# Splits of reloaded activations and weights given to POOL, a later combination step, ACT-issued stores and an 18th operand place in a float32 transformer block

## The chip, the cores and the metric

The kernel runs on one core of a Trainium2 chip. The metric is the time of one execution in device microseconds (us). Engines are named as in the profile: PE multiplies matrices (PEld loads its stationary operand), DVE, ACT and POOL work elementwise, SP only issues DMAs, each engine has its own in-order queue.

## The reference, cut to what matters

One decoder block over 2048 tokens of width 1024, in float32:

```python
h = rmsnorm(x, norm_pre_mix);  proj = h @ w_in        # q, k, v, u, z, gate_a, gate_b
y_attn = dilated_attention(rope(q), rope(k), v)       # 3 dilations x 4 heads, softmax over the 3 results
y_gmlp = gelu(u) * spatial_mix(layernorm(gelu(z)))
merged = sigmoid(gate_a) * (y_attn @ w_branch_attn) + sigmoid(gate_b) * (y_gmlp @ w_branch_gmlp)
x = x + rmsnorm(merged @ w_out, norm_post_mix)
h = rmsnorm(x, norm_pre_mlp)
x = x + rmsnorm(relu(h @ w_mlp_in)**2 @ w_mlp_out, norm_post_mlp)
```

## The kernel before, in words

**Precision by splitting.** Each float32 operand is split into a high part (a copy rounded to the type that PE takes, fp32r) and a low part (the operand minus the high part), and a product is three matmuls: high by high, high by low, low by high (`mm3`, lines 94 to 97). The helper `split` (line 67) makes the two parts: the high one on ACT (line 70) or on POOL (line 72), the low one by a subtraction on DVE or POOL (line 78, or line 85 where it was put off until behind a product). `split_in` (line 87) first issues the load from SP (line 91).

**Order of the work.** PE's order is as the program writes it. The order of ACT, DVE, POOL and SP is set by a planner with its own costs, except in the first products of the MLP and from the end of its first stage on (`as_written`): there they too run in the order written. Queues are strictly in order: an instruction that waits holds back everything behind it on its engine.

**The attention stretch.** The projections u, z and the gates g are cut into steps (one step: the three matmuls of one k-tile, for 512 tokens), and a generator `filler` (line 474) hands these steps out between the pieces of 48 attention units, some nine steps a unit (line 714 on). Each unit: scores on PE, masked maximum on DVE, `nm` on DVE (line 604), exponentials on ACT (line 607), transposes on PE, their split `ph` by ACT and DVE (lines 632, 633), `pf` by ACT (line 640), the product `pv` on PE (line 646). The steps need hT, the transposed activations of a chunk of 512 tokens (two buffers, four chunks). Chunks 0 and 1 were written to DRAM and come back by `reload_h` (line 212), at the gate columns n = 7 of the second half and n = 0 of the first: four loads, each 128x1024, each split in a high part on ACT and a low one on DVE. The weights w of a column come by `load_w` (line 221): two raw tiles (two buffers), high part on POOL, low part on DVE.

**The combination.** After the last unit, `combine(c)` (line 657) weighs the three attention results of each chunk, in the order c = 2, 3, 0, 1: loads A (two buffers), small work on DVE, a multiplication on DVE (line 681), two additions of 128x1024 (lines 683 and 684; on DVE for c = 2, else on POOL), transposes on PE (line 689), a copy on ACT and a store of 'ya' (one buffer). Between the chunks PE runs 30, 20, 17 and 13 steps of the filler (line 745). When the last chunk's transposes are out, the space goes to wb, the branch weights, needed by the merge.

**The MLP, first stage.** It is computed by Strassen-Winograd products over pairs of hidden tiles q: seven products i = 1..7 instead of eight (`product`, line 1005). Sums of the weights by POOL (`add_a`, lines 987 to 990) are split by `split_a` into seven rotating buffers, in the order WL: yt0, yt1, yt2, gmlp, yt3, yt4, yt5. In the first products some yt tiles still hold sums of transposed activations (tt) on their way to DRAM (td). The results are squared and stored to s_d by `store_s` (line 1021): while `store_eng` is SP (the first products, lines 1170 to 1227), the store is issued from SP; later from ACT.

**The MLP, second stage.** Eight groups g of two pairs q; each group has eight blocks of tokens, each block seven products of six matmuls (`yproduct`, line 1545). A product uses an operand (B11, B21, T2, T3, T1, T4, B22: numbers 0 to 6) of both q's, split by `op_w2` (line 1295: high on ACT, low on POOL) into one of 17 rotating places of 128x2x512. Within a block's period the order on PE is: i=1 (operand 0), the block before's i=7 (3) and i=5 (4), i=2 (1), i=6 (2), the block before's i=4 (5) and i=3 (6). The next group's operand 0 is made in block nth = 3, POOL's sums of its raw weights in nth = 4 (`sum_w2`, six subtractions) and in the last block (`sum_w2_last`, two), and its operands 1 to 6 in the last block, operand u+1 after the product that last uses operand u (line 1604). POOL also forms four sums of the stored s per block (lines 1354 to 1357), ACT and DVE split them.

Of the kernel before, what the change touches and what calls it, by code (L numbers as in the profile page):

```python
# [8 lines left out]
F32 = mybir.dt.float32  # L9
F32R = mybir.dt.float32r  # L10
# [31 lines left out]
def block_kernel(ctx, tc, a, out):  # L42
# [169 lines left out]
    def reload_h(c):  # L212

        hT[c] = hp.tile([P, 2, KT, 512], F32R, name=f"hT_b{c}", tag="hT", bufs=2)
        for k in range(0, KT, 2):
            split_in(hT[c][:, :, k:k + 2], hT_d[c, :, k:k + 2, :], None, "act")

    def w_src(i, kk):
        return a["w_in"][i, :, kk * 4:(kk + 1) * 4, :]

    def load_w(i, name):

        w = wp.tile([P, 2, 2, 4, 256], F32R, name=name, tag="w", bufs=3)
        for kk in range(2):
            raw = wp.tile([P, 4, 256], F32, name=f"{name}_r{kk}", tag="raw", bufs=2)
            split_in(w[:, kk], w_src(i, kk), raw)
        return [w[:, 0], w[:, 1]]

    def wide_tiles(name):
# [236 lines left out]
    def want(q):  # L466
        if q < len(queue) and q not in loaded:
            wi, kind, n, half = queue[q]
            if kind == "z":
                loaded[q] = None if n else load_wide(wi, f"w_z{half}")  # L470
            else:
                loaded[q] = load_w(wi, f"w_{kind}{n}{half}")

    def filler():

# [181 lines left out]
    def combine(c):  # L657

        A = cb.tile([P, 4, 3, 264], F32, name=f"A_{c}", tag="cA", bufs=2)
        for g in range(3):  # L660
            sp.dma_start(A[:, :, g, :], att_d[g][c * 512:(c + 1) * 512, :].rearrange("(n p) e -> p n e", p=P))
        yield
        M = sm.tile([P, 4, 4], F32, name=f"M_{c}", tag="cM")
        dve.tensor_max(M, A[:, :, 0, 260:264], A[:, :, 1, 260:264])
        dve.tensor_max(M, M, A[:, :, 2, 260:264])
        E = sm.tile([P, 4, 3, 4], F32, name=f"E_{c}", tag="cE")
        for g in range(3):
            dve.tensor_sub(E[:, :, g, :], A[:, :, g, 260:264], M)
        act.activation(E, E, AF.Exp, scale=0.125)
        Z = sm.tile([P, 4, 3, 4], F32, name=f"Z_{c}", tag="cZ")  # L670
        for g in range(3):
            dve.tensor_mul(Z[:, :, g, :], E[:, :, g, :], A[:, :, g, 256:260])
        dve.tensor_add(M, Z[:, :, 0, :], Z[:, :, 1, :])
        dve.tensor_add(M, M, Z[:, :, 2, :])
        dve.reciprocal(M, M)
        for g in range(3):
            dve.tensor_mul(E[:, :, g, :], E[:, :, g, :], M)
        for i in range(4):
            for g in range(3):
                o = A[:, i, g, 0:256].rearrange("p (j e) -> p j e", j=4)  # L680
                dve.tensor_tensor(o, o, widen(E[:, i, g, :], 64), op=OP.mult)
        eng = dve if c == 2 else pool
        eng.tensor_add(A[:, :, 0, :256], A[:, :, 0, :256], A[:, :, 1, :256])
        eng.tensor_add(A[:, :, 0, :256], A[:, :, 0, :256], A[:, :, 2, :256])
        yield
        for m in range(2):
            pt = psum_aux(f"yt_{c}{m}")
            for i in range(4):
                pe.transpose(pt[:, i * P:(i + 1) * P], A[:, i, 0, m * P:(m + 1) * P], ident)
            yt = cb.tile([P, 512], F32, name=f"ya_{c}{m}", tag="cya", bufs=1)  # L690
            act.activation(yt, pt, AF.Copy)
            sp.dma_start(ya_d[m, :, c * 512:(c + 1) * 512], yt)
        yield
# [48 lines left out]
        next(cs[n])  # L742
        next(cs[n])
    for n in range(4):
        steps((30, 20, 17, 13)[n])
        next(cs[n])
        if n < 2:
            next(cs[n + 2])
            next(cs[n + 2])
# [255 lines left out]
    def product(half, q, i):  # L1005
# [13 lines left out]


        def store_s(o, t):
            (act if store_eng is None else store_eng).dma_start(s_d[q, half][:, :, o, :], t.rearrange("p (i c) -> p i c", i=4))

        def square(t, src):
            act.activation(t, src, AF.Relu)
# [267 lines left out]
        w2r_[q] = raw  # L1293

    def op_w2(q, name, lo_eng):
        w = spots[n_op[0] % 17]
        n_op[0] += 1
        raw = w2r_[q][:, dict(B11=0, B12=1, B21=2, T2=4, T3=1, T1=0, T4=2, B22=3)[name]]
        split(w[:, 0], w[:, 1], raw, "act", lo_eng)
        w2_[q, name] = w  # L1300

    def sum_w2(q, part):
# [59 lines left out]
            split(w[:, 0, :, to], w[:, 1, :, to], raw[:, :, k], "act", "dve")  # L1362
            yield

    def ops_of(g, j, lo_eng="pool"):
        ops = OPS if g < NQ // 2 - 1 else PLAIN_OPS
        for q in (2 * g, 2 * g + 1):
            if j < len(ops):
                op_w2(q, ops[j], lo_eng)

    last_ones = order[n_last:]

    def fours(name):
        w = bp.tile([P, 4, 2, 512], F32R, name=f"{name}_spots", tag=name, bufs=1)
        spots.extend(w[:, k] for k in range(4))

    in_order = behind()
    in_order.enter_context(as_written())
# [4 lines left out]
    for n, z in enumerate(last_ones):  # L1383
        if n == 0:
            for w in range(2):
                load_w2(w)
            load_s(0)
            load_s(1)
            split_a(h, q - 1, "S2", "S3")
        elif n == 1:  # L1390
            split_a(h, q - 1, "S1")
        elif n == 2:
            split_a(h, q - 1, "A22")
            add_a(h, q)
        elif n == 3:
            split_a(h, q - 1, "S4")
        elif n == 5:
            split_a(h, q, "S2")
        elif n == 6:
            split_a(h, q, "S3", "S1")  # L1400
        elif n == 7:
            split_a(h, q, "A22")
            next(s0)
        elif n == 8:
            split_a(h, q, "S4")
            rest()
            next(s0)
        elif n == 9:
            ew.close()
            s1p = stack(e3, "s1p", 1)  # L1410
            sm = stack(e3, "sm3", 2)
            acc0 = s1p.tile([P, D], F32, name="acc0")
            spots.append(s1p.tile([P, 2, 512], F32R, name="spot0"))
            fours("T2")
            for j in range(2):
                ops_of(0, j, "dve")
        elif n == 10:
            for part in (0, 1):
                for w in range(2):
                    sum_w2(w, part)  # L1420
            next(s0)
        elif n == 11:
            next(s0)
            rest()
            load_s(2)
        elif n == 12:
            fours("T3")
            ops_of(0, 2, "dve")
            next(s1)
        elif n == 13:  # L1430
            fours("T1")
            ops_of(0, 3, "dve")
            next(s1)
            for w in range(2):
                sum_w2_last(w)
        elif n == 14:
            fours("T4")
            ops_of(0, 4, "dve")
# [88 lines left out]
    def plain(n, k):  # L1527
# [7 lines left out]
        for m, q in enumerate((2 * g, 2 * g + 1)):  # L1535
            s, w = st_[n][:, :, m, at_], w2_[q, name]
            for o, (l, r) in enumerate(((0, 0), (0, 1), (1, 0))):
                pe.matmul(p, s[:, l], w[:, r], start=not t and not m and not o, stop=t == 1 and m == 1 and o == 2,
                          skip_group_check=True)
        if t:  # L1540
            an = acc[half, b, ci][:, nh * 512:(nh + 1) * 512]
# [3 lines left out]
    def yproduct(n, i):  # L1545
# [7 lines left out]
        for m, q in enumerate((2 * g, 2 * g + 1)):  # L1553
            s, w = st_[n][:, :, m, S_AT[i]], w2_[q, name]
            for o, (l, r) in enumerate(((0, 0), (0, 1), (1, 0))):
                pe.matmul(p, s[:, l], w[:, r], start=i in (1, 2, 5) and not m and not o, stop=m == 1 and o == 2,  # L1556
                          skip_group_check=True)
        ci, nh = {1: (0, 0), 2: (0, 0), 6: (0, 1), 3: (0, 1), 4: (1, 0), 7: (1, 1), 5: (1, 1)}[i]
        an = acc[half, b, ci][:, nh * 512:(nh + 1) * 512]
# [23 lines left out]
    for k, (_, n, i) in enumerate(yorder):  # L1583
# [4 lines left out]
        else:  # L1588
            yproduct(n, i)
        if not n and i in (1, 2):  # L1590
            ops_of(0, 4 + i, "dve")
# [113 lines left out]
```

## Time and profile before

| | |
|---|---|
| runs shown | 2780.45, 2775.97, 2776.09 us; median 2776.09 |
| profiled execution | 2779.44 us, its span 2777.7 us |
| PE busy | 2712.0 us of the span (98%) |
| DVE, ACT, POOL busy | 1545.2, 1051.9, 947.3 us |
| mean granted clock of PE | 0.991 |

Times of rows count from the span's start. A row of the timeline has start, duration, engine, line, operation, out<-in, shape, count, and in brackets the idle time of the engine before it and what ended that. A row of the waits has the total, the number and the longest of the waits. A row of the windows has the stretch, its length, then busy time and number of instructions for PE, PEld, DVE, ACT, POOL, the mean granted clock of PE (1.00 is full), and the share and rate of the DMA engines.

### The profile page before, as it was taken

To read this page: it belongs to the slowest core of one execution; us is meant where nothing else is said; L and a number is where in the kernel's file an instruction comes from. 1 tells how busy PE (TensorE), PEld (TensorE's weight loads), DVE (VectorE), ACT (ScalarE), POOL (GpSimd) and SP (SyncE) were. 2 spreads that over 40 slices of the span, in tenths; PEclk is the share of its full clock that TensorE was granted. 3 is DMA by queue.
4 is the path that set the end of the run, shared out by engine and by line. 5 is a ranking of instruction groups with operands and counts; after the bars stand their busy time and mean duration, and the time that the engine had idled before them with its cause. 6 is when DMAs were issued, how large, how long until landed. Compare 5 with 4: busy or idle time off the path is not lost. (4 is left out here: it accounts for less than half of the span.)

```text
span 2777.7 us, 34732 instructions
## 1 busy us (share of the span) xinstructions
PE 2712.0 (98%) x12668; PEld 2242.3 (81%) x12668; DVE 1545.2 (56%) x2643; ACT 1051.9 (38%) x2151; POOL 947.3 (34%) x777
## 2 busy tenths in 40 slices
PE   9999999999999999999999999999999999999998
PEld 7888888888878887787787788878887887777787
DVE  5655552344453344554556644555436777777766
ACT  5213111244453321354444544555444333233334
POOL 0341341200000013312215432223314766677645
PEclk9999999999999999999999999999999999999999
DMA  7445455466666654655658534554343122222236
GB/s 266 168 145 169 156 152 195 126 190 195 193 217 192 190 166 149 186 190 160 183 171 268 168 103 125 181 168 126 106 146 108 54 84 84 84 84 84 84 106 213
DMA packets 298380, 426.00 MB, mean 153 GB/s; under 512 B 18528, under 2 KB 172384, under 8 KB 298208
## 3 DMA queue, kind: packets, MB, share of 16 engines
q1 hardware_dynamic: 210368, 372.12, 42.3%
q10 hardware_dynamic: 87840, 51.65, 6.2%
q8 instruction: 100, 1.64, 0.2%
q14 instruction: 72, 0.59, 0.1%
HBM read 282.99 MB, written 140.71 MB: 153 GB/s over the span
## 5 line engine op out<-in xcount | busy, mean ns | idle before, releaser
L1556 PE MATMUL ya<-T_spots,s 128*128 128x512 f32 x1272 | 313.1, 392 | 4.8 <-DVE acc L1564 2.7
L1556 PEld LDWEIGHTS ya<-T_spots,s 128*128 128x128 f32 x1272 | 239.0, 188 | 59.0 <-issue 4.5
L70 ACT ACTIVATE s<-sraw 128x768 fp32r<-128x768 f32 (+1 forms) x184 | 126.0, 695 | 358.2 <-POOL sraw L1355 199.0
L1016 PE MATMUL aa<-B,A 128*128 128x512 f32 x768 | 187.0, 396 | 6.3 <-ACT xs L1030 5.1
L78 DVE TENSOR_TENSOR s<-sraw,s 128x512 fp32r<-128x512 f32 x171 | 163.6, 979 | 34.6 <-ACT s L70 33.0
L987 POOL TENSOR_TENSOR s<-w1r 128x512 f32<-128x512 f32 x32 | 43.5, 1359 | 397.3 <-DVE S L78 337.3
L1016 PEld LDWEIGHTS aa<-B,A 128*128 128x128 f32 x768 | 145.5, 190 | 40.5 <-ACT xs L1030 6.0
L72 POOL TENSOR_SCALAR w_g<-w_g_r 128x1024 fp32r<-128x1024 f32 x32 | 34.1, 1082 | 412.3 <-PE g L97 313.7
L1556 PE MATMUL yc<-T_spots,s 128*128 128x512 f32 x624 | 164.1, 394 | 3.6 <-POOL T_spots L78 3.6
L95 PE MATMUL x<-hT_a,wq 128*128 128x512 f32 x384 | 149.7, 390 | 0.0
L97 PE MATMUL x<-hT_a,wq 128*128 128x512 f32 x384 | 149.4, 389 | 0.0
L96 PE MATMUL x<-hT_a,wq 128*128 128x512 f32 x384 | 149.4, 389 | 0.0
L1556 PEld LDWEIGHTS yc<-T_spots,s 128*128 128x128 f32 x624 | 115.8, 188 | 33.6 <-POOL T_spots L78 9.7
L653 DVE TENSOR_REDUCE o<-po 128x256 f32<-128x512 f32 x48 | 33.1, 690 | 187.5 <-PE po L652 187.5
L78 POOL TENSOR_TENSOR T_spots<-w2r,T_spots 128x512 fp32r<-128x512 f32 x86 | 123.2, 1459 | 5.4 <-ACT T_spots L70 5.4
L70 ACT ACTIVATE hl<-r 128x512 fp32r<-128x512 f32 x48 | 30.4, 633 | 233.2 <-POOL r L287 89.0
L95 PE MATMUL g<-hT_b,w_g 128*128 128x512 f32 x256 | 105.0, 410 | 0.0
L95 PE MATMUL g<-hT_a,w_g 128*128 128x512 f32 x256 | 104.8, 409 | 0.0
L95 PE MATMUL o<-wo,mg 128*128 128x512 f32 x256 | 100.8, 394 | 4.1 <-ACT mg L70 4.1
L70 ACT ACTIVATE S<-w1r 128x512 fp32r<-128x512 f32 x96 | 60.0, 629 | 112.0 <-PE ac L1016 66.6
L815 POOL TENSOR_TENSOR g<-g,g 128x512 f32<-128x512 f32 x28 | 38.8, 1385 | 185.9 <-DVE g L813 179.2
L1354 POOL TENSOR_TENSOR sraw<-sraw 128x256 f32<-128x256 f32 x56 | 41.3, 737 | 174.6 <-DVE s L78 160.3
(379 smaller groups left out, 7214.4 us busy)
## 6 DMA issues: line engine op xcount, KB each, us to landing
w1r<-in_w_mlp_in_dram SPq DMA_DIRECT2D x64, 512.0 KB, 3.6
sraw<-sd SPq DMA_DIRECT2D x128, 256.0 KB, 3.4
qk<-hl SPq DMA_DIRECT2D x24, 1024.0 KB, 5.4
qq<-qk SPq DMA_DIRECT2D x96, 256.0 KB, 5.1
w_g_r<-in_w_in_dram SPq DMA_DIRECT2D x32, 512.0 KB, 5.3
gated<-gt SPq DMA_DIRECT2D x64, 256.0 KB, 3.4
g<-gated SPq DMA_DIRECT2D x64, 256.0 KB, 4.4
w2r<-in_w_mlp_out_dram SPq DMA_DIRECT2D x16, 1024.0 KB, 6.0
```

The lines of the kernel that those rows point to most:

```text
L70: act.activation(hi, src, AF.Copy)
L72: pool.tensor_scalar(hi, src, 1.0, 1.0, op0=OP.mult, op1=OP.mult)
L78: (pool if lo_eng == "pool" else dve).tensor_sub(lo, src, f32(hi))
L95: pe.matmul(ps, lh, rh, start=start, stop=False)
L96: pe.matmul(ps, lh, rl, start=False, stop=False)
L97: pe.matmul(ps, ll, rh, start=False, stop=stop)
L653: dve.tensor_reduce(ot[:, :, j * 64:(j + 1) * 64], po.rearrange("p (b h e) -> p b e h", b=4, h=2), axis=AX.X, op=OP.add)
L815: (dve if dt == KT - 1 else pool).tensor_add(parts[0], parts[0], parts[1])
L987: pool.tensor_add(s1, a21, a22)
L1016: pe.matmul(p, w[:, l, k, :], h[:, r, k, :], start=i in (1, 6, 5) and not k and not n, stop=k == 3 and n == 2, skip_group_check=True)
L1354: pool.tensor_add(a22, a21, a22)
L1556: pe.matmul(p, s[:, l], w[:, r], start=i in (1, 2, 5) and not m and not o, stop=m == 1 and o == 2, skip_group_check=True)
```

## The change

- `reload_h`: high and low part of the four pieces on POOL (were ACT and DVE).
- `load_w`: for the gate columns n = 0 and 1 of the first half, the low part on POOL too.
- `combine`: the two additions of chunk 1 on DVE (were on POOL); two buffers for 'ya'; the steps between the chunks are 33, 21, 20 and 24.
- `WL` begins with gmlp; the order is then yt0, yt1, yt2, yt3, yt4, yt5.
- `store_s` always issues from ACT.
- Second stage: an 18th place (two tiles of the buffers xs); operands 0 and 1 of the next group in block nth = 3; its eight sums in nth = 4 (one q) and nth = 5 (the other), none in the last block; in the last block operand u+2 after the last use of operand u; the low part of the first q on DVE for the operands made behind i = 2 and i = 7 (operands 3 and 5).

```diff
         for k in range(0, KT, 2):
-            split_in(hT[c][:, :, k:k + 2], hT_d[c, :, k:k + 2, :], None, "act")
+            split_in(hT[c][:, :, k:k + 2], hT_d[c, :, k:k + 2, :], None, "pool", "pool")
...
-    def load_w(i, name):
+    def load_w(i, name, lo_eng="dve"):
...
-            split_in(w[:, kk], w_src(i, kk), raw)
+            split_in(w[:, kk], w_src(i, kk), raw, "pool", lo_eng)
...
-                loaded[q] = load_w(wi, f"w_{kind}{n}{half}")
+                loaded[q] = load_w(wi, f"w_{kind}{n}{half}", "pool" if (kind, half) == ("g", 0) and n < 2 else "dve")
...
-        eng = dve if c == 2 else pool
+        eng = dve if c in (1, 2) else pool
...
-            yt = cb.tile([P, 512], F32, name=f"ya_{c}{m}", tag="cya", bufs=1)
+            yt = cb.tile([P, 512], F32, name=f"ya_{c}{m}", tag="cya", bufs=2)
...
-        steps((30, 20, 17, 13)[n])
+        steps((33, 21, 20, 24)[n])
...
-    WL, n_wl = ("yt0", "yt1", "yt2", "gmlp", "yt3", "yt4", "yt5"), [0]
+    WL, n_wl = ("gmlp", "yt0", "yt1", "yt2", "yt3", "yt4", "yt5"), [0]
...
-            (act if store_eng is None else store_eng).dma_start(s_d[q, half][:, :, o, :], t.rearrange("p (i c) -> p i c", i=4))
+            act.dma_start(s_d[q, half][:, :, o, :], t.rearrange("p (i c) -> p i c", i=4))
...
-        w = spots[n_op[0] % 17]
+        w = spots[n_op[0] % len(spots)]
...
-    def ops_of(g, j, lo_eng="pool"):
+    def ops_of(g, j, lo_engs=("pool", "pool")):
         ops = OPS if g < NQ // 2 - 1 else PLAIN_OPS
-        for q in (2 * g, 2 * g + 1):
+        for q, eng in zip((2 * g, 2 * g + 1), lo_engs):
             if j < len(ops):
-                op_w2(q, ops[j], lo_eng)
+                op_w2(q, ops[j], eng)
...
+    spots.append([rx.tile([P, 512], F32R, name=f"spot_{n}", tag="xs", bufs=LEAD + 1) for n in range(2)])
...
             if nth == 3:
                 ops_of(g + 1, 0)
-            if nth == 4 and g + 1 < NQ // 2 - 1:
+                ops_of(g + 1, 1)
+            if nth in (4, 5) and g + 1 < NQ // 2 - 1:
+                w = 2 * g + nth - 2
                 for part in (0, 1):
-                    for w in (2 * g + 2, 2 * g + 3):
-                        sum_w2(w, part)
+                    sum_w2(w, part)
+                sum_w2_last(w)
...
-        if more and nth == len(blocks) - 1 and USE[i][0] < 6:
-            ops_of(g + 1, USE[i][0] + 1)
-            if i == 1 and g + 1 < NQ // 2 - 1:
-                for w in (2 * g + 2, 2 * g + 3):
-                    sum_w2_last(w)
+        if more and nth == len(blocks) - 1 and USE[i][0] < 5:
+            ops_of(g + 1, USE[i][0] + 2, ("dve" if i in (2, 7) else "pool", "pool"))
```

The other changed lines only carry a place as a pair of tiles instead of one tile.

More of the change, by code (lines that the diff above doesn't have):

```diff
@@ L1295, in op_w2 @@
     def op_w2(q, name, lo_eng):
-        w = spots[n_op[0] % 17]
+        w = spots[n_op[0] % len(spots)]
         n_op[0] += 1
         raw = w2r_[q][:, dict(B11=0, B12=1, B21=2, T2=4, T3=1, T1=0, T4=2, B22=3)[name]]
-        split(w[:, 0], w[:, 1], raw, "act", lo_eng)
+        split(*w, raw, "act", lo_eng)
         w2_[q, name] = w
@@ L1374, in fours @@
         w = bp.tile([P, 4, 2, 512], F32R, name=f"{name}_spots", tag=name, bufs=1)
-        spots.extend(w[:, k] for k in range(4))
+        spots.extend((w[:, k, 0], w[:, k, 1]) for k in range(4))
     in_order = behind()
@@ L1412, in block_kernel @@
             acc0 = s1p.tile([P, D], F32, name="acc0")
-            spots.append(s1p.tile([P, 2, 512], F32R, name="spot0"))
+            w = s1p.tile([P, 2, 512], F32R, name="spot0")
+            spots.append((w[:, 0], w[:, 1]))
             fours("T2")
             for j in range(2):
-                ops_of(0, j, "dve")
+                ops_of(0, j, ("dve", "dve"))
         elif n == 10:
@@ L1427, in block_kernel @@
             fours("T3")
-            ops_of(0, 2, "dve")
+            ops_of(0, 2, ("dve", "dve"))
             next(s1)
@@ L1431, in block_kernel @@
             fours("T1")
-            ops_of(0, 3, "dve")
+            ops_of(0, 3, ("dve", "dve"))
             next(s1)
@@ L1437, in block_kernel @@
             fours("T4")
-            ops_of(0, 4, "dve")
+            ops_of(0, 4, ("dve", "dve"))
             next(s1)
@@ L1537, in plain @@
             for o, (l, r) in enumerate(((0, 0), (0, 1), (1, 0))):
-                pe.matmul(p, s[:, l], w[:, r], start=not t and not m and not o, stop=t == 1 and m == 1 and o == 2,
+                pe.matmul(p, s[:, l], w[r], start=not t and not m and not o, stop=t == 1 and m == 1 and o == 2,
                           skip_group_check=True)
@@ L1555, in yproduct @@
             for o, (l, r) in enumerate(((0, 0), (0, 1), (1, 0))):
-                pe.matmul(p, s[:, l], w[:, r], start=i in (1, 2, 5) and not m and not o, stop=m == 1 and o == 2,
+                pe.matmul(p, s[:, l], w[r], start=i in (1, 2, 5) and not m and not o, stop=m == 1 and o == 2,
                           skip_group_check=True)
@@ L1590, in block_kernel @@
         if not n and i in (1, 2):
-            ops_of(0, 4 + i, "dve")
+            ops_of(0, 4 + i, ("dve", "dve"))
         if i == 1 and more:
```

## The prediction

> **What bounds the kernel now.** First the page's busy times:
>
> ```profile
> PE 2712.0 (98%) x12668; PEld 2242.3 (81%) x12668; DVE 1545.2 (56%) x2643; ACT 1051.9 (38%) x2151; POOL 947.3 (34%) x777
> ```
>
> PE is the bound: nothing of its work is removed, so only its idle 2% and the time that it runs at a lower clock can be won. Then the waits of PE (who ended them; total, number, longest), and the windows of the four stretches that the change touches:
>
> ```profile
> PE yt L689 <- POOL A L684: 5.1, 1, 5.1
> ...
> PE yc L1556 <- POOL T_spots L78: 3.6, 5, 0.7
> ...
> PE pv L646 <- ACT ph L632: 2.7, 1, 2.7
> ...
> PE ya L1556 <- DVE acc_yt L1561: 2.1, 6, 0.4
> ```
>
> ```profile
> 765.00:800.00 35.00, 28.60 (x146) 24.14 (x145) 19.97 (x36) 19.61 (x46) 2.06 (x2) 0.90 0.71 234
> ...
> 1065.00:1080.00 15.00, 9.91 (x40) 8.11 (x39) 6.36 (x4) 1.68 (x3) 9.10 (x5) 0.77 0.44 139
> ...
> 1505.00:1545.00 40.00, 32.12 (x116) 23.83 (x116) 27.53 (x25) 21.63 (x33) 20.47 (x12) 0.87 0.85 273
> 2136.00:2755.00 619.00, 612.58 (x2661) 497.58 (x2660) 449.83 (x615) 202.80 (x381) 413.50 (x390) 1.00 0.30 97
> ```
>
> Length less PE busy is PE's idle time: 6.4, 5.1, 7.9 and 6.4 us. The clock column adds a second loss: after the first three PE ran part of the time at half clock; 0.90 of 35 us is 7 us at half. Of these stretches' half-speed time the part that falls into the wait itself is not lost again, so I count 3.0, 2.0 and 4 us. In all about 35 us are to be had.
>
> **A. Reload in the attention stretch** (`reload_h`, `load_w`).
>
> ```profile
> 765.81 1.06 ACT L70 ACTIVATE hT_b<-hT_b 128x1024 fp32r<-128x1024 f32 x1 [1.80 <-DMA hT_b<-hTd]
> ```
>
> ```profile
> 783.18 0.39 PE L95 MATMUL g<-hT_b,w_g 128*128 128x512 f32 x1
> ```
>
> ```profile
> 790.43 0.40 PE L95 MATMUL g<-hT_b,w_g 128*128 128x512 f32 x1
> ```
>
> ```profile
> 803.71 0.39 PE L95 MATMUL g<-hT_b,w_g 128*128 128x512 f32 x1
> ```
>
> ACT's four high parts stand among a unit's exponentials, `ph` comes late, PE waits for `pv`; but the first reload is not used before 783.18, its last quarter at 790.43, and the second, by the count of steps, at 803.71. With the splits on POOL this wait has no cause: +9.4 us (6.4 idle, 3.0 clock). POOL's price for a piece is one high part and one low:
>
> ```profile
> 744.05 2.06 POOL L72 TENSOR_SCALAR w_g<-w_g_r 128x1024 fp32r<-128x1024 f32 x2 [31.63 <-PE g L97]
> 783.43 2.06 POOL L72 TENSOR_SCALAR w_g<-w_g_r 128x1024 fp32r<-128x1024 f32 x2 [37.33 <-DMA qq<-qk]
> ```
>
> ```profile
> 1064.16 3.59 POOL L683 TENSOR_TENSOR A<-A 128x1024 f32<-128x1024 f32 x1 [4.49 <-DVE A L681]
> 1067.73 1.04 POOL L72 TENSOR_SCALAR w_z<-w_z_r 128x1024 fp32r<-128x1024 f32 x1
> 1068.73 2.34 POOL L684 TENSOR_TENSOR A<-A 128x1024 f32<-128x1024 f32 x1
> 1071.04 2.02 POOL L72 TENSOR_SCALAR wb<-wbraw 128x1024 fp32r<-128x1024 f32 x1
> ```
>
> That is 1.04 + 2.4 = 3.45 us beside an idle DVE, 2.02 + 3.59 = 5.6 beside a busy one. POOL is otherwise empty there. Ten pieces stand in a row: four of the first reload from 765.8 (where ACT gets the first now), two of the weights that now come at 783.43, four of the second reload. They end at 765.8 + 34.5 = 800.3. Needed: the first reload 6.7 us earlier than now, since 3.7 us of waits (2.7 of them the row of `ph`) and the 3.0 of slow clock before 783.18 are gone: from 776.5, last quarter 7.2 us on at 783.7; POOL has it at 779.6. The second 803.71 - 783.18 = 20.5 us later, less the stretch's other 2.7 us of waits: from 794.3, last quarter at 801.5. So POOL is in time by 1 us if the weights go first, and by more if not. What it may cost is DVE:
>
> ```profile
> 744.32 0.80 DVE L604 TENSOR_SCALAR nm<-o 128x4 f32<-128x4 f32 x1
> ```
>
> ```profile
> 753.93 0.17 DVE L604 TENSOR_SCALAR nm<-o 128x4 f32<-128x4 f32 x1
> ```
>
> ```profile
> 757.32 0.28 ACT L640 ACTIVATE pf<-pT 128x128 f32<-128x128 f32 x1 [0.49 <-DVE ph L633]
> ```
>
> ```profile
> 759.01 0.39 PE L646 MATMUL pv<-pf,v 128*128 128x128 f32 x2
> ```
>
> `nm` took 0.80 instead of 0.17 beside POOL's split, ending as POOL's first instruction did. Behind POOL's 2.4 us it can wait that long; exponentials, `ph` and `pf` queue behind it, and `pf` (done 757.60) has 1.4 us until PE uses it at 759.01. So at most 1.0 a unit, in five units, and only if it meets the wrong phase: 0.7 us. [...] SP's queue: raw tiles of these weights come free some 5 us later, SP's next weight loads with them; units' loads run two units ahead and hide it. I take +8; the ends are +9.4 and the rival below.
>
> **B. Combination.**
>
> ```profile
> 1043.66 1.04 PE L689 MATMUL yt<-ident,A 128*128 128x128 f32 x8
> ```
>
> ```profile
> 1026.52 1.22 DVE L683 TENSOR_TENSOR A<-A 128x1024 f32<-128x1024 f32 x1
> ```
>
> ```profile
> 1002.94 0.39 PE L97 MATMUL g<-hT_b,w_g 128*128 128x512 f32 x1
> ...
> 1003.62 0.39 PE L97 MATMUL g<-hT_b,w_g 128*128 128x512 f32 x1
> ```
>
> The chain that ends the 5.1 us wait: chunk 3's transposes (1043.66) free the buffer A, chunk 1 loads, DVE multiplies, POOL adds from 1064.16 to 1071.07: 27.4 us. Two adds on DVE take 2.4, and one weight split may stand between (1.2): done by about 1068, 24.4 us. PE's cover was 17 + 13 steps of 0.68 us (1002.94 to 1003.62) and two transposes, 22.4; it becomes 20 + 24 steps, 32. The wait goes, with 7 us to spare: +7.1 (5.1 idle, 2.0 clock); chunk 0 gets 41 steps where 37 sufficed. The second 'ya' buffer only frees ACT. Ending later costs the branch weights 18 steps, 12 us less the 5 saved:
>
> ```profile
> L78 DVE TENSOR_TENSOR wb<-wbraw,wb x6: 1225/1226/1227, 1073.1 to 1094.7; 128x1024 fp32r<-128x1024 f32 x6
> ```
>
> ```profile
> 1132.70 0.40 PE L95 MATMUL b<-yt,wb 128*128 128x512 f32 x1
> ```
>
> They were ready 37 us before use; hidden. I take +7 (5 to 7.5).
>
> **C. First products of the MLP** (`WL`, `store_s`).
>
> ```profile
> 1506.32 0.63 ACT L70 ACTIVATE S<-w1r 128x512 fp32r<-128x512 f32 x1 [1.39 <-DMA td<-tt]
> ...
> 1514.07 0.60 ACT L1025 ACTIVATE c<-aa 128x512 f32<-128x512 f32 x1 [4.38 <-DMA sd<-c]
> ...
> 1517.85 0.63 ACT L70 ACTIVATE A<-ar 128x512 fp32r<-128x512 f32 x1 [0.63 <-DMA ar<-in_w_mlp_in_dram]
> ```
>
> ```profile
> 1507.00 0.73 PE L1016 MATMUL ab<-T_first,S 128*128 128x512 f32 x2 [1.12 <-ACT S L70]
> ...
> 1519.02 1.22 PE L1016 MATMUL aa<-B,A 128*128 128x512 f32 x2 [3.99 <-ACT xs L1030]
> 1521.48 4.54 PE L1016 MATMUL aa<-B,A 128*128 128x512 f32 x10 [1.23 <-DVE A L85]
> ```
>
> ```profile
> 1510.63 0.91 SPq L946 DMA_DIRECT2D ar<-in_w_mlp_in_dram  x1
> ```
>
> ```profile
> 1543.75 0.54 ACTq L1022 DMA_DIRECT2D sd<-u  x1
> ```
>
> S in gmlp no longer waits for a td store (1.39), and c no longer for SP to get to its store (4.38). But then the product of 1519.02 is held by its weights: 'ar' lands at 1517.8, 7.2 us after its issue, with the DMA engines 0.85 busy, and that stays. PE reaches this product earlier and waits longer; its low part is done near 1519.5 instead of 1521.4. Seven stores on ACT cost 0.54 each, 3.8 us, most of it in ACT's gaps. I take +2. Ends: -3.8 (no store hidden) and +10 (nothing waits, clock included).
>
> ```profile
> 1509.00:1512.00 3.00, 3.00 (x8) 2.31 (x7) 2.43 (x2) 0.63 (x1) 1.89 (x2) 0.50 0.93 285
> ```
>
> Half clock follows already on the 1.5 us wait of 1507 (1.12 and 0.38). [...]
>
> **D. Second stage.**
>
> ```profile
> 2201.21 3.00 POOL L1314 TENSOR_TENSOR w2r<-w2r 128x512 f32<-128x512 f32 x2
> ...
> 2213.87 8.73 POOL L78 TENSOR_TENSOR T_spots<-w2r,T_spots 128x512 fp32r<-128x512 f32 x6
> ```
>
> At each change of group POOL has twelve low parts of 1.46 us (six of them in the 8.73 us) and two sums of 1.5 close behind one another; PE waits 0.72 for operand 4, and 0.35 as the late s sums hold DVE. Six changes of group: 6.4 us, at full clock. After: eight low parts, no sums, and operand 4 four slots earlier: 4 x 1.46 + 3.0 = 8.8 us less, against 0.72. The two low parts on DVE wait 0.6 us for ACT there. Blocks 3, 4 and 5 now hold four low parts, four and four sums: 6 us each in a block of 9.7, where before block 4 held six sums, 9; hidden. +6 (3 to 6.4).
>
> **Sum.** 8 + 7 + 2 + 6 = 23. From the profiled 2779.4 that is 2756.4; this execution lies 3.3 above the median of the runs, 2776.1, so I forecast **2753**.
>
> **Rivals.**
> - *POOL becomes the bound in the attention stretch* (slower). If every piece costs 5.6 as beside a busy DVE, the tenth ends at 821.8, 20 us late, with 3.4 for half clock (6.8 us of it after the wait) and six units' `nm` held 3.59 - 1.4 = 2.2 each (13): A is 9.4 - 36.6 = -27, the sum -12: **2788**. It eats the whole gain from a piece of 4.7 us on (11 late, 3.4, and six times 1.6: A is -15, what B, C and D bring). For: the 3.59 row. Against: DVE has few two-input jobs there once these splits are gone. 0.08. [...]
> - *The second reload is a little late*: pieces of 4.0 us, 4.6 us late and half clock: A near 0, **2761**. For: a margin of 1 us. 0.12.
> - *ACT pays for the stores*: C at -3.8, **2759**. 0.07.
> - *The early products gain in full*, 'ar' landing earlier once two stores leave SP's queue ahead of it: C +10, **2745**. Against: the DMA engines are busy either way. 0.10.
> - *The waits only change their owner* (DVE's low parts hold the sums in D, planner's order undoes A): B alone, less new half-clock time, **2772**. 0.08.
>
> **Numbers.** The forecast, 2748 to 2758, has 0.55. Range 2744 to 2767: the four nearest cases; it leaves out 0.16 and little else. What a measurement here tells from no change is about 0.2%, 5.5 us: faster 0.84, within 0.08, slower 0.08.
>
> **What would show it.** A: no wait for `pv` near 770 and 795, POOL's ten pieces near 3.5 us, hT ready before use. B: no wait for yt. C: no wait for td or sd on ACT, one longer wait for 'ar'. D: no 0.7 waits of yc. Wrong if POOL's low parts take over 4 us, if PE waits for hT, or if the granted clock falls in a place where it is 1.00 now.

## The result, and the profile after

The changed kernel takes 2753.64 us (median of five runs, 2750.45 to 2756.65), the kernel before 2780.42 (median of five, 2775.97 to 2780.65): a ratio of 0.9907, 95% interval 0.9896 to 0.9917. The forecast was 2753.0. That it is met so closely is partly luck, as shown below: the terms of the sum came to 23 us, the change is worth 26 (25.8 by the profiled spans, 26.8 by the medians), and I had taken 3 us off for a base that was not there. The ratios here are of fast executions: three slow ones among those below, one of the kernel before (3827.9 us), one of C alone (6945.34) and one of D alone (3712.83), are left out of them.

The profiled execution of the changed kernel took 2753.64 us, its span 2751.9; that of before 2779.44 and 2777.7. So the spans differ by 25.8 us, and these are what the following rows have to account for. The page's busy times of the changed kernel:

```profile
PE 2699.0 (98%) x12668; PEld 2237.4 (81%) x12668; DVE 1558.8 (57%) x2646; ACT 1050.3 (38%) x2145; POOL 965.5 (35%) x782
```

PE has the same 12668 matmuls in 13 us less of busy time: half of the gain lies inside busy time; the other half is idle time. Of PE's busy time 38.65 us lay at half clock before and 20.22 after, by estimate 9 of the 13 us, counting a microsecond at half clock as half lost (in the changed kernel, matmuls of `g` start 0.43 us apart at 786.53 and 0.23 at 788.48); the rest I put down, as an estimate too, to pauses too short to count as idle, like those in a row of 1.79 us for six matmuls that take 1.52 elsewhere. The windows of the four stretches, first before, then after (columns as above; the combination before stands in the prediction; the third and the fourth window lie 13 and 14 us earlier after the change, as the work in them does):

```profile
757.00:800.00 43.00, 36.60 (x194) 31.16 (x193) 23.05 (x48) 21.68 (x50) 2.06 (x2) 0.92 0.70 224
...
1503.00:1553.00 50.00, 42.12 (x159) 32.01 (x158) 34.58 (x36) 27.70 (x43) 25.25 (x16) 0.90 0.85 278
2125.00:2744.00 619.00, 609.91 (x2643) 494.95 (x2642) 453.70 (x620) 204.81 (x375) 411.39 (x388) 1.00 0.30 96
```

```profile
757.00:800.00 43.00, 39.55 (x220) 33.99 (x219) 17.80 (x50) 17.47 (x54) 31.15 (x18) 0.96 0.76 239
1065.00:1080.00 15.00, 15.00 (x72) 12.52 (x71) 6.89 (x7) 2.28 (x4) 4.40 (x2) 1.00 0.53 179
1490.00:1540.00 50.00, 42.61 (x172) 32.90 (x171) 37.57 (x38) 30.16 (x48) 26.01 (x17) 0.93 0.79 267
2111.00:2730.00 619.00, 615.73 (x2690) 504.67 (x2689) 485.49 (x641) 212.98 (x393) 398.95 (x380) 1.00 0.30 99
```

Read them stretch by stretch: the combination (second row after) has no idle time and full clock; in the attention stretch (first) 3.45 us of idle time and a clock of 0.96 are left; in the first products of the MLP (third) 7.4 of 7.9 us of idle time are left, in three listed waits instead of six; in the second stage idle time fell from 9.1 to 3.3 us.

Where the time came from is read best from one and the same instruction in both timelines. Three such pairs, the first of each pair from before, the second from after:

```profile
808.72 0.69 DVE L653 TENSOR_REDUCE o<-po 128x256 f32<-128x512 f32 x1 [3.98 <-PE po L652]
...
1088.27 0.39 PE L95 MATMUL z<-w_z,hT_b 128*128 128x512 f32 x1
...
2138.33 0.85 PE L1556 MATMUL yc<-T_spots,s 128*128 128x512 f32 x3
```

```profile
803.27 0.69 DVE L653 TENSOR_REDUCE o<-po 128x256 f32<-128x512 f32 x1 [3.46 <-PE po L652]
...
1074.83 0.39 PE L95 MATMUL z<-w_z,hT_b 128*128 128x512 f32 x1
...
2122.65 1.54 PE L1558 MATMUL yc<-T_spots,s 128*128 128x512 f32 x6
```

Behind the attention stretch the changed kernel is 5.45 us ahead, behind the combination 13.44, early in the second stage 15.68, at the end 25.8. Part A gave 5.4 (forecast 8), B 8.0 (7), what lies between z and the second stage 2.2 (C was 2), D 10.1 (6).

The same rows in the other traces tell which of these numbers are the part's own. B's 8.0 and D's 10.1 come again, to 0.1 us, in every trace of a kernel with that part. A's 5.4 does not: in three of the other traces with the same A the reduction stands at 804.10 (a second trace of the changed kernel), 801.87 and 805.20 (the two runs under "Pieces of B and D", the second first), a lead of 4.6, 6.8 and 3.5 us. Nor are the 2.2 us C's own. The lead is 14.24 us ahead of the first products of the MLP (`pt`, line 868, at 1475.79 and 1461.55) and 16.18 behind them (`ac`, line 1016, at 1558.24 and 1542.06), so 1.9 us were won there; by the same rows it is 0.4 us in a second trace of the changed kernel and -0.3 in the run with C alone.

### The profile page after: what moved, and what is told of

Same layout as the page of the kernel before. It is cut to its first block, busy times and chain, and to the rows that moved or that the text cites. A ratio compares the mean times of both kernels' runs of the same rounds, so it can differ in the third digit from the quotient of the medians.

```text
span 2751.9 us, 34711 instructions
## 1 busy us (share of the span) xinstructions
PE 2699.0 (98%) x12668; PEld 2237.4 (81%) x12668; DVE 1558.8 (57%) x2646; ACT 1050.3 (38%) x2145; POOL 965.5 (35%) x782
## 5 line engine op out<-in xcount | busy, mean ns | idle before, releaser
L1558 PE MATMUL ya<-T_spots,s 128*128 128x512 f32 x1176 | 291.6, 391 | 3.3 <-DVE acc L1566 3.3
L1558 PEld LDWEIGHTS ya<-T_spots,s 128*128 128x128 f32 x1176 | 220.7, 188 | 52.3 <-ACT T_spots L70 3.1
L78 DVE TENSOR_TENSOR s<-sraw,s 128x512 fp32r<-128x512 f32 x171 | 179.6, 1075 | 7.1 <-ACT s L70 7.0
L78 POOL TENSOR_TENSOR T_spots<-w2r,T_spots 128x512 fp32r<-128x512 f32 x70 | 104.6, 1521 | 7.5 <-ACT T_spots L70 7.5
```

Source lines behind the costliest of these rows:

```text
L78: (pool if lo_eng == "pool" else dve).tensor_sub(lo, src, f32(hi))
L1558: pe.matmul(p, s[:, l], w[r], start=i in (1, 2, 5) and not m and not o, stop=m == 1 and o == 2, skip_group_check=True)
```

## Experiments

### Each part alone

**A alone.** The kernel before with `reload_h` and `load_w` as in the change:

```diff
-            split_in(hT[c][:, :, k:k + 2], hT_d[c, :, k:k + 2, :], None, "act")
+            split_in(hT[c][:, :, k:k + 2], hT_d[c, :, k:k + 2, :], None, "pool", "pool")
...
-                loaded[q] = load_w(wi, f"w_{kind}{n}{half}")
+                loaded[q] = load_w(wi, f"w_{kind}{n}{half}", "pool" if (kind, half) == ("g", 0) and n < 2 else "dve")
```

> The kernel before with part A alone (splits of the reload on POOL, low parts of gate columns 0 and 1 of the first half on POOL). Theory 1, four separate waits: the whole gain of A is 5.3 us (the idle time and slow clock near 770 and 795 less a new wait of PE for the transposes of a unit of 3.4 us near 784), so 2775 against 2780, and no other place of the trace moves. Theory 2, the parts need one another (the earlier steps of A are lost again at the combination, where the filler's steps cover a wait): 0 to 2 us, and the wait for yt longer than 5.1.

Measured: 2776.09 us against 2780.3, ratio 0.9988 (0.9980 to 0.9997). Of its waits of PE:

```profile
PE pT L627 <- DVE o L653: 5.0, 2, 4.3
PE yt L689 <- POOL A L684: 4.6, 1, 4.6
```

The new wait for the transposes (`pT`, 4.3 us here) is A's own, and the wait of the combination stays as it was: theory 1, with a gain at the lower end of what its trace says (the reduction of the row above stands at 804.16, 4.6 us earlier than before).

**B alone.**

```diff
-        eng = dve if c == 2 else pool
+        eng = dve if c in (1, 2) else pool
...
-            yt = cb.tile([P, 512], F32, name=f"ya_{c}{m}", tag="cya", bufs=1)
+            yt = cb.tile([P, 512], F32, name=f"ya_{c}{m}", tag="cya", bufs=2)
...
-        steps((30, 20, 17, 13)[n])
+        steps((33, 21, 20, 24)[n])
```

> The kernel before with part B alone (two additions of chunk 1 on DVE, two buffers for ya, steps 33, 21, 20, 24). Theory 1: 8 us less, 2772; no wait for yt, clock 1.00 between 1065 and 1080, the first product with the branch weights 8 us earlier. Theory 2, the 24 steps held back only move the wait to the branch weights or the first merge: 0 to 4 us, with a longer wait for g or wb behind it.

Measured: 2771.1 us, ratio 0.9969 (0.9957 to 0.9981). The window of the combination:

```profile
1065.00:1080.00 15.00, 15.00 (x72) 12.53 (x71) 13.91 (x30) 5.08 (x9) 5.88 (x2) 1.00 0.55 178
```

No idle time, full clock; theory 1.

**C alone.**

```diff
-    WL, n_wl = ("yt0", "yt1", "yt2", "gmlp", "yt3", "yt4", "yt5"), [0]
+    WL, n_wl = ("gmlp", "yt0", "yt1", "yt2", "yt3", "yt4", "yt5"), [0]
...
-            (act if store_eng is None else store_eng).dma_start(s_d[q, half][:, :, o, :], t.rearrange("p (i c) -> p i c", i=4))
+            act.dma_start(s_d[q, half][:, :, o, :], t.rearrange("p (i c) -> p i c", i=4))
```

> The kernel before with part C alone (WL begins with gmlp, first stores from ACT). Theory 1: 2 us less, inside what one kernel's runs scatter; one wait of about 5.7 us for xs near 1515 (ACT held by the landing of 'ar') in place of waits of 1.1, 4.0 and 1.2. Theory 2, the saving in C needs the other parts: no less than 0.5 us different from before.

Measured: 2777.64 us, ratio 0.9989 (0.9980 to 0.9998). One long wait for xs, 6.6 us, as expected, but waits for S of 0.8 twice are left in this run. The trace shows no saving at the place of C: it is 1.4 us ahead of the kernel before when the first products begin and 1.1 behind them. What the interval allows, 0.6 to 5.6 us, is thus not shown to be C's.

**D alone.** The second stage's part of the change, on the kernel before; its core:

```diff
-        w = spots[n_op[0] % 17]
+        w = spots[n_op[0] % len(spots)]
...
+                ops_of(g + 1, 1)
...
-            ops_of(g + 1, USE[i][0] + 1)
+            ops_of(g + 1, USE[i][0] + 2, ("dve" if i in (2, 7) else "pool", "pool"))
```

> The kernel with part D alone (second stage: 18th place, operands 0 and 1 and the sums early, two low parts on DVE). Theory 1, the trace's own account by periods of blocks: 10 us less, 2770, since a change of group costs 1.9 us before and nothing after, less 0.035 us a block. Theory 2, the sum of the listed waits, as I predicted: 6 us less, 2774, and the other 4 come from somewhere else (the end of the first stage, A to C).

Measured: 2769.09 us, ratio 0.9962 (0.9949 to 0.9975), that is 11 us: the account by periods, not the sum of the listed waits. The four ratios fall short of 1 by 0.12, 0.31, 0.11 and 0.38%, together 0.92%; the whole change by 0.93%. As far as intervals of about 0.1% each can tell, the parts are independent, and the rival that waits only change their owner is out.

### What is left of A

The wait of 3.4 us that the changed kernel has in the attention stretch, in its timeline (DVE, POOL, PE, in this order):

```profile
780.29 4.04 DVE L78 TENSOR_TENSOR w_g<-w_g_r,w_g 128x1024 fp32r<-128x1024 f32 x2 [4.79 <-POOL w_g L72]
784.25 0.68 DVE L653 TENSOR_REDUCE o<-po 128x256 f32<-128x512 f32 x1
```

```profile
779.21 2.06 POOL L72 TENSOR_SCALAR w_g<-w_g_r 128x1024 fp32r<-128x1024 f32 x2
781.24 2.01 POOL L72 TENSOR_SCALAR hT_b<-hT_b 128x1024 fp32r<-128x1024 f32 x1
783.33 3.21 POOL L78 TENSOR_TENSOR hT_b<-hT_b 128x1024 fp32r<-128x1024 f32 x1
...
794.65 2.40 POOL L78 TENSOR_TENSOR hT_b<-hT_b 128x1024 fp32r<-128x1024 f32 x1
```

```profile
784.98 0.90 PE L627 MATMUL pT<-ident,e 128*128 128x128 f32 x3 [3.44 <-DVE o L653]
```

Two low parts of weights took DVE 4.04 us instead of 3.18 before, side by side with POOL's splits of the second reload, which took 2.01 and 3.21 instead of 1.04 and 2.4. The reduction stands behind them in DVE's queue, PE's transposes wait for it. It stood there before too, and PE did not wait:

```profile
784.52 3.18 DVE L78 TENSOR_TENSOR w_g<-w_g_r,w_g 128x1024 fp32r<-128x1024 f32 x2 [1.66 <-POOL w_g L72]
787.63 0.68 DVE L653 TENSOR_REDUCE o<-po 128x256 f32<-128x512 f32 x1
```

The 0.9 us by which the low parts became longer are the smaller part of the wait. PE begins these transposes 7.3 us earlier than before (780.94 against 788.28), the two low parts only 4.2 us earlier (780.29 against 784.52): their high parts stood in POOL's queue behind the first reload, whose last piece ended at 779.2. The experiment takes those two low parts to POOL as well:

```diff
-"pool" if (kind, half) == ("g", 0) and n < 2 else "dve"
+"pool" if (kind, half) == ("g", 0) and n < 3 else "dve"
```

> The changed kernel with the low parts of gate column n = 2 on POOL too (n < 3 in place of n < 2): the ten pieces in a row that my prediction counted. Theory 1 (what is left of A's gain is lost to DVE, whose two weight splits took 4.04 us beside POOL's and stand ahead of the reduction that PE's transposes wait for): the wait of 3.4 us and the half clock behind it go, 4 to 5 us less than the changed kernel, about 2749; POOL's tenth piece ends near 800 against a need of 801.5. Theory 2 (POOL is then late): PE waits for hT near 796 to 800, and the time is that of the changed kernel or up to 4 us more.

Measured: 2748.95 us, ratio to before 0.9883 (0.9866 to 0.9899). Window, POOL, DVE and the same reduction as above:

```profile
757.00:800.00 43.00, 42.97 (x251) 37.15 (x250) 18.04 (x55) 18.25 (x55) 33.82 (x20) 1.00 0.87 273
```

```profile
781.52 4.76 POOL L78 TENSOR_TENSOR w_g<-w_g_r,w_g 128x1024 fp32r<-128x1024 f32 x2
```

```profile
781.57 2.37 DVE L604 TENSOR_SCALAR nm<-o 128x4 f32<-128x4 f32 x1
...
798.73 0.69 DVE L653 TENSOR_REDUCE o<-po 128x256 f32<-128x512 f32 x1 [2.71 <-PE po L652]
```

PE is busy for all 43 us at full clock, and the reduction comes 4.54 us earlier than in the changed kernel: theory 1. The row of `nm` shows POOL's price: an instruction that takes 0.17 us at 800.69 took 2.37 here, beside POOL's low part of 781.52. Nothing waited for it long enough to be seen on PE.

**Low parts of the reload on DVE.** The other way to relieve the meeting of the two engines:

```diff
-            split_in(hT[c][:, :, k:k + 2], hT_d[c, :, k:k + 2, :], None, "pool", "pool")
+            split_in(hT[c][:, :, k:k + 2], hT_d[c, :, k:k + 2, :], None, "pool", "dve")
```

> The changed kernel with the eight low parts of the reload back on DVE, the high ones staying on POOL. Theory 1 (DVE's queue is what PE waits for in this stretch, so work must leave DVE, not only ACT): DVE has 8 x 1.22 to 2.05 us more in the units; the wait for the transposes (3.4) comes back longer or at more places, 2 to 6 us more than the changed kernel, 2756 to 2760. Theory 2 (ACT's high parts alone made the old waits, the low parts may be anywhere): within 1 us of the changed kernel, or 1 to 3 us less since POOL's instructions that block DVE are shorter.

Measured: 2758.28 us (2754.16 to 2759.22), ratio 0.9916 (0.9901 to 0.9930), an interval that overlaps that of the changed kernel. The profiled run is the fastest of the four; its window and waits:

```profile
757.00:800.00 43.00, 39.92 (x225) 33.63 (x224) 26.61 (x59) 17.55 (x54) 12.63 (x10) 1.00 0.81 245
```

```profile
PE pT L627 <- DVE o L653: 2.3, 2, 1.7
PE pv L646 <- DVE ph L633: 1.5, 2, 1.2
```

In the stretch it loses as much as the changed kernel (3.1 us idle against 3.45), in two shorter waits and without half clock; its reduction stands at 802.68, 0.6 us earlier. Theory 2 holds for the stretch. The median falls into the 2756 to 2760 of theory 1, but nothing in the trace speaks for it; whether the median's 4.6 us more are real, and where they would lie, stays open. Against the ten pieces the picture is clear: the low parts belong on POOL, if all of them go there.

### What is left of C

In the changed kernel, PE and ACT at the one long wait:

```profile
1504.17 5.26 PE L1016 MATMUL aa<-B,A 128*128 128x512 f32 x12 [5.70 <-ACT xs L1030]
```

```profile
1503.01 0.63 ACT L70 ACTIVATE A<-ar 128x512 fp32r<-128x512 f32 x1 [5.99 <-DMA ar<-in_w_mlp_in_dram]
```

PE is said to wait for xs, but xs (1503.54) stands behind the split of 'ar' on ACT, and that waited for a load issued at 1494.77. Two experiments. The first has the order WL alone, on the kernel before:

```diff
-    WL, n_wl = ("yt0", "yt1", "yt2", "gmlp", "yt3", "yt4", "yt5"), [0]
+    WL, n_wl = ("gmlp", "yt0", "yt1", "yt2", "yt3", "yt4", "yt5"), [0]
```

> The kernel before with WL alone (stores still from SP). Theory 1 (the wait for S is WL's, the waits of ACT for sd are the stores'): the 1.1 us wait for S goes, ACT still waits some 4 us for sd ahead of c, PE's wait for xs stays near 4 to 5 us with the 1.2 behind it: 0 to 1 us less than before. Theory 2 (the order of WL carries all of C): the waits are those of the run with both parts of C.

Measured, one run: 2780.92 us. PE and ACT:

```profile
1520.02 1.22 PE L1016 MATMUL aa<-B,A 128*128 128x512 f32 x2 [7.75 <-ACT xs L1030]
```

```profile
1515.05 0.60 ACT L1025 ACTIVATE c<-aa 128x512 f32<-128x512 f32 x1 [7.97 <-DMA sd<-c]
```

The wait for S is gone and the wait behind it as much longer: ACT sits 7.97 us on a store that SP has not got to. WL alone is worth nothing; it needs the stores from ACT. That is theory 1, with the wait for xs longer than expected.

The second issues 'ar' ahead of two loads of 512 KB, on the changed kernel (the split that frees its buffer moves with it):

```diff
+        split_lone(h, 3, 0)
+        raw_lone(h, 4, 1)
         load_a(h, 1)
         add_a(h, 0)
         split_t(h, "T2", (2,))
-        split_lone(h, 3, 0)
...
         begin(3, 1)
-        raw_lone(h, 4, 1)
```

> The changed kernel with the load of 'ar' (weights of the product that waits 5.7 us) issued ahead of the two loads w1r of 512 KB each instead of behind them. Theory 1 (what is left of C is the landing of 'ar' behind 1 MB in the DMA queue, not ACT's stores): ar lands 4 to 5 us earlier, the wait falls from 5.7 to about 1.5 and half of its slow clock goes: 4 to 7 us less, about 2748. Theory 2 (the DMA engines are full, what is late only changes its name): the products behind wait for S of the later w1r by as much, within 2 us of the changed kernel.

Measured: 2749.95 us (2749.43 to 2750.82), ratio to before 0.9889 (0.9874 to 0.9904). The same product, and ACT's split:

```profile
1502.61 3.01 PE L1016 MATMUL aa<-B,A 128*128 128x512 f32 x12 [1.23 <-ACT xs L1030]
```

```profile
1501.44 0.63 ACT L70 ACTIVATE A<-ar 128x512 fp32r<-128x512 f32 x1 [3.06 <-DMA ar<-in_w_mlp_in_dram]
```

The wait falls from 5.70 to 1.23 and the half clock behind it goes (the granted clock is 1.00 from 1500 to 1508; in the changed kernel it was 0.50 from 1501.65 to 1508.47), but my size of the cause was wrong: issue to use fell from 8.2 us (1494.77 to 1503.01) to 6.3 (1495.18 to 1501.44), 2.0 us and not 4 to 5. The rest came from PE, which in this run reached the product 2.9 us later, after a wait for S of 1.23 and 0.50 us that starts earlier and is no part of the edit (a second trace of the changed kernel has one of 0.69 and 0.47). The medians differ by 3.7 us, with intervals that touch (0.9874 to 0.9904 here, 0.9896 to 0.9917 for the changed kernel: the last run below bears the gain out); that the two loads alone make it is not shown.

### Pieces of B and D

**Additions of chunk 1 back on POOL**, the steps and the buffer as in the change:

```diff
-        eng = dve if c in (1, 2) else pool
+        eng = dve if c == 2 else pool
```

> The changed kernel with the two additions of chunk 1 back on POOL, all else of B kept. Theory 1 (the chain of 27.4 us ends inside the cover of 20 + 24 steps and two transposes, 32 us, so the steps alone remove the wait): no wait for yt, clock 1.00 between 1065 and 1080, time within 1 us. Theory 2 (the additions on DVE are needed): a wait for yt of 2 to 4 us.

Measured, one run: 2757.69 us. The window of the combination and POOL's last addition:

```profile
1065.00:1080.00 15.00, 15.00 (x72) 12.52 (x71) 6.12 (x11) 2.89 (x5) 6.93 (x4) 1.00 0.56 194
```

```profile
1070.27 2.40 POOL L684 TENSOR_TENSOR A<-A 128x1024 f32<-128x1024 f32 x1
```

The addition ends at 1072.7, and no transpose waits for it: theory 1 for the place. (The time is 4 us above the changed kernel's median in a single run; the same reduction as above stands at 805.20, 1.9 us later, so half of it was lost ahead of the combination, where the edit changes nothing; half clock lasts 6.83 us there instead of 3.41, as the last section shows.) B's gain from the reduction to z is 8.0 us here too. The 32 us of cover carry B, with the second 'ya' buffer, which no run took away; the move of the additions to DVE carries nothing.

**Low parts of operands 3 and 5 back on POOL:**

```diff
-            ops_of(g + 1, USE[i][0] + 2, ("dve" if i in (2, 7) else "pool", "pool"))
+            ops_of(g + 1, USE[i][0] + 2, ("pool", "pool"))
```

> The changed kernel with the low parts of operands 3 and 5 back on POOL (ten low parts of 1.3 to 1.5 us behind one another at a change of group instead of eight). Theory 1 (place 18, the early operands and the early sums carry D; ten low parts are 14 us against the 9.6 us of a block, but each has four slots more): period of a block at a change of group at most 9.7 us as now, time within 1 us. Theory 2 (the split of the work between POOL and DVE carries D): a wait for POOL's low parts of 0.5 to 3 us at each of six changes, 3 to 12 us more.

Measured, one run: 2753.61 us. The first matmul of the same product in four blocks around a change of group, in the kernel before, the changed kernel, and this one (first and last of the four):

```profile
2210.88 1.52 PE L1556 MATMUL yc<-T_spots,s 128*128 128x512 f32 x6
...
2221.59 1.79 PE L1556 MATMUL yc<-T_spots,s 128*128 128x512 f32 x6
...
2232.08 1.54 PE L1556 MATMUL yc<-T_spots,s 128*128 128x512 f32 x6
...
2241.67 1.52 PE L1556 MATMUL yc<-T_spots,s 128*128 128x512 f32 x6
```

```profile
2204.85 1.54 PE L1558 MATMUL yc<-T_spots,s 128*128 128x512 f32 x6
...
2214.48 1.54 PE L1558 MATMUL yc<-T_spots,s 128*128 128x512 f32 x6
...
2224.09 1.52 PE L1558 MATMUL yc<-T_spots,s 128*128 128x512 f32 x6
...
2233.71 1.54 PE L1558 MATMUL yc<-T_spots,s 128*128 128x512 f32 x6
```

```profile
2204.83 1.54 PE L1558 MATMUL yc<-T_spots,s 128*128 128x512 f32 x6
...
2233.70 1.54 PE L1558 MATMUL yc<-T_spots,s 128*128 128x512 f32 x6
```

The periods: 10.71, 10.49, 9.59 before; 9.63, 9.61, 9.62 after; together 28.86 us after and 28.87 here. A change of group cost 10.71 + 10.49 - 2 x 9.59 = 2.0 us (the other five 1.9 to 2.1 by the same count) and costs nothing now, with ten low parts on POOL as with eight: theory 1. The split of low parts between POOL and DVE carries nothing.

### Both mends together

The two edits above, `n < 3` and 'ar' first, in one kernel, and the changed kernel again beside it:

> Both mends together: the changed kernel with the low parts of gate column n = 2 on POOL and 'ar' issued ahead of the two w1r. Theory 1 (the two places are separate): the gains add, 4.7 and 3.7 us, 2745 against 2753.6 of the changed kernel. Theory 2 (PE comes 4.7 us earlier to the first products of the MLP and waits there for the same landing): 2749, no better than either alone.

> The changed kernel itself, once more, beside the kernel with both mends: 2751 to 2756, and the mends' gain can then be read on one chip.

Measured on one chip: 2745.48 us (2743.68 to 2747.37) with both mends, 2755.14 (2752.84 to 2757.27) for the changed kernel; ratios to before 0.9872 (0.9855 to 0.9888) and 0.9908 (0.9894 to 0.9923). That is 9.7 us less where 8.4 were expected: the gains add as far as the intervals can tell, theory 1, and the version is faster than both kernels. Its windows:

```profile
757.00:800.00 43.00, 43.00 (x254) 37.29 (x253) 15.11 (x57) 18.03 (x55) 33.73 (x20) 1.00 0.84 273
...
1490.00:1540.00 50.00, 45.19 (x179) 35.13 (x179) 41.56 (x42) 31.02 (x49) 29.47 (x20) 0.93 0.80 263
```

The attention stretch has nothing left. In the first products 4.8 us of idle time remain, the longest waits being 2.26 for xs and 2.20 for S.

## Why the prediction was right

**The base was wrong, and hid an error in the sum.** I took 3.3 us off because the profiled execution lay above the median of three runs, 2776.1. Later series put the kernel before at 2780.42, 2780.3, 2779.86 and 2780.99: the profiled 2779.4 was the typical run, and two of the three runs shown were low ones. Without that step I would have forecast 2756.4, 2.8 us too high, because the sum of the parts was 23 and not 26.

**A, forecast 8, measured 5.4.** POOL's prices were right (3.45 a piece, the second reload done at 794.65 + 2.40 = 797.1, in time) and `pv`'s waits went. What failed is the step "ten pieces in a row" with "DVE has few two-input jobs there once these splits are gone". I gave the weights of 783.43 to columns 0 and 1; weights are split as soon as one of three buffers is free, two columns ahead of their use, so these are column 2's (the run with `n < 3` moves just them), whose low parts the edit leaves on DVE. The rows that I missed are those of DVE before, 784.52 and 787.63: two low parts of 3.18 us directly ahead of a reduction on PE's path. I asked when POOL's pieces are needed as operands, and not what stands behind them on DVE: PE came 7.3 us earlier and these low parts, held by POOL's row of pieces, 4.2, and beside POOL's longer occupation they took 4.04 us. With them on POOL the chain of ten pieces is as I described it, and A comes to 5.4 + 4.5 = 9.9, above my upper end of 9.4. POOL as the bound, the rival of 2788, did not come: only one piece took more than 3.5 us (2.01 + 3.21, the one beside DVE's weights). One of the prediction's signs of being wrong did appear: the clock is 0.50 from 784.85 on, where it was 1.00 before. The other two, low parts of over 4 us on POOL and a wait for hT, did not.

**DVE beside POOL.** At the places shown above both engines took longer side by side: DVE's `nm` 2.37 us instead of 0.17 (with `n < 3`), two low parts on DVE 4.04 instead of 3.18, POOL's pieces 2.01 instead of 1.04 and 3.21 instead of 2.4. On PE the price was not the 0.7 us for `nm` that I took, and not one for every unit: the one wait in which the longer rows had a share is that of 3.4 us with 3.41 us of half clock behind it, of which the longer low parts make 0.9 and the queue the rest.

**B, forecast 7, measured 8.0.** The reasoning by the cover (22.4 us against a chain of 27.4, then 32) was right, and the run with the additions on POOL shows that they were not needed. The term was 1 us short; 0.6 of it is a wait of 0.59 us at the first chunk's transposes (1029.10 before), which I did not count and which the changed kernel does not have.

**C, forecast 2, measured 0 to 2.** No wait of ACT for sd, the product held by 'ar' in one longer wait of 5.7: as forecast. That the waits for td on ACT and for S on PE go was not borne out. The profiled run has 0.42 and 0.28 us of the first and none of the second, but a second trace of the changed kernel has ACT 3.67 us on td and PE 0.69 and 0.47 us on S. With gains of 1.9, 0.4 and -0.3 us at this place in three traces, the agreement of the term with 2.2 is luck. The two loads ahead of 'ar' in the queue were not in my account; with 'ar' issued first, issue to use is 6.3 us instead of 8.2 and the median 3.7 us lower.

**D, forecast 6, measured 10.1.** The mechanism was right, the size came from the wrong view. I added the waits that the list of waits names, 0.72 and 0.35 us for six changes of group. The periods of blocks show 2.0 us for each change, about 12 in all, less 0.03 us that every block now takes longer (9.62 against 9.59; 56 blocks, 1.7 us): 10.4, against 10.1 measured, in the run with D alone too. The rest of the loss stood in durations, as in the row of 1.79 us for six matmuls that take 1.52 elsewhere: pauses too short to be listed as waits. The cause of the 0.03 us was not tried.

## What to carry to other kernels

Where a loop has a period, price its disturbances by the period, not by the listed waits: here the list showed half of the loss. When splits move from one elementwise engine to another, list what the first still has to do in the same microseconds and what stands behind that in its queue: here two low parts on DVE, 4.04 us beside POOL instead of 3.18, stood ahead of a reduction that PE waited 3.4 us for. A term read from one trace can be luck: those of B and D came again in every trace, those of A and C did not. And a base of three runs can be 4 us off; a sum made from the profiled execution should be set against it with that much doubt.

## What was not expected of the hardware

Half clock does not follow from the length of a wait alone. PE's wait for the transposes near 785 is 3.44 us in the changed kernel, 3.47 in the run with the low parts of operands 3 and 5 back on POOL, and 4.17 in the run with the additions of chunk 1 back on POOL. Behind it PE has half clock for 3.41 us, not at all, and for 6.83 us. In these traces the clock changes only at points that lie a whole number of 3.41 us apart. Cut at these points, the wait falls into two stretches of each run (two rows a run, in this order; the last column but two is the clock):

```profile
781.44:784.85 3.41, 0.09 (x1) 0.00 (x0) 3.41 (x4) 0.60 (x1) 3.33 (x2) 1.00 0.82 323
784.85:788.26 3.41, 3.28 (x10) 2.71 (x11) 2.28 (x11) 1.65 (x7) 3.33 (x3) 0.50 0.70 204
```

```profile
779.88:783.29 3.41, 1.73 (x13) 1.31 (x11) 2.89 (x2) 0.60 (x1) 3.41 (x3) 1.00 1.02 387
783.29:786.71 3.42, 1.63 (x9) 1.41 (x10) 3.39 (x12) 0.00 (x0) 3.34 (x3) 1.00 0.52 196
```

```profile
780.71:784.12 3.41, 1.31 (x9) 0.89 (x7) 2.60 (x2) 0.60 (x1) 3.41 (x3) 1.00 1.02 393
784.12:787.54 3.42, 1.35 (x5) 1.25 (x6) 3.39 (x11) 0.00 (x0) 3.34 (x2) 0.50 0.32 121
```

In these runs it goes with how much of a stretch PE is idle. It is idle for 3.32 us and then for 0.13 in the first run, for 1.68 and 1.79 in the second, whose third stretch has a clock of 1.00 too, and for 2.10 and 2.07 in the third, whose third stretch has 0.50. All 14 traces together have 11135 such stretches at full clock: with PE idle for less than 0.43 of the stretch (10991 of them) half clock never followed, with more than 0.56 (98) it always did, and between these it did in 8 of 46 (the traces of the kernel before and the changed kernel alone: 0 of 1569, 14 of 14, 2 of 9). It ended behind all 91 stretches at half clock with less than 0.09 idle, and behind none of the 64 with more than 0.2 (in those two traces 14 of 14 and 0 of 9).

So short waits that share a stretch can cost half clock, like the 1.23 and 0.50 us at 1493 and 1494 in the run with 'ar' first (the clock is 0.50 from 1496 to 1498), and a longer one that is cut by a boundary may cost none, like the 3.47 us above. The boundaries differ from run to run (784.85, 783.29 and 784.12 in the three above), so a prediction should carry both cases: with 0, 3.41 and 6.83 us of half clock behind this one wait, A's lead was 6.8, 5.4 and 3.5 us.
